# Another order for the pieces of a mixing block: equal turns and alternating quarters

## The chip, the cores and the metric

The kernel runs on one core of one Trainium2 chip. A core has a matrix engine (TensorE, "PE" in the profile; "PEld" is its weight load, which overlaps the matmuls), a vector engine (VectorE, "DVE"), an activation engine (ScalarE, "ACT"), a general engine (GpSimd, "POOL") and SyncE ("SP"), whose queue issues the DMA transfers here. The engines run side by side and wait for each other through semaphores. The metric is device microseconds of one execution, smaller is better.

## The reference, cut to what matters

A sequence of 512 tokens of width 1024 goes through two models' blocks. The first block has a mixing part and a mixture of experts; two attention layers with feed-forward parts follow. The edit concerns only the mixing part of the first block, which has two branches on the same normalised input `h`:

```python
a_x, a_gate, hy, gates = jnp.split(h @ w_in[l], [...], axis=-1)
xa = dwconv(a_x, conv_a_w[l], ...)
h_a = rg_lru(xa, ..., False) + rg_lru(xa, ..., True)
y_a = (h_a * gelu(a_gate)) @ w_a_out[l]
v, x1, x2 = jnp.split(dwconv(hy, conv_b_w[l], ...), 3, axis=-1)
filt = hyena_filters(S, ...)
z = v
for n, gate in enumerate((x1, x2)):
    z = gate * fftconv(z, bidir_kernel(filt[:, n, 0], filt[:, n, 1]), filt_bias[l, n])
y_b = z @ w_b_out[l]
g_a, g_b = jnp.split(sigmoid(gates), 2, axis=-1)
x = x + (g_a * y_a + g_b * y_b) @ w_o[l]
```

Branch A is a gated linear recurrence in both directions. Branch B multiplies spectra twice: a long convolution over the sequence with a filter, a gate, a second long convolution, a second gate. `g_a` and `g_b` are the sixteen output gates, 128 columns each.

## The kernel before, in words

Activations lie with channels on the partitions, 128 channels by 512 tokens a tile. A projection (`proj`, line 952) makes one such tile from `h`: eight blocks of 128 input channels, each with three matmuls of 128x512 (`mm3`, lines 163 to 165), since every f32 operand is split into a high and a low half (`hh`, `hl` of the input, `wh`, `wl` of the weight) and high x high, high x low and low x high are summed. `WStream.get` (line 217) loads the weight by DMA into one of three raw buffers (line 228), ScalarE copies the high half (line 152), DVE subtracts it to get the low half (line 155); there are two buffers of each half. Three PSUM banks take projections.

The code of the mixing part walks two lists of short words.

List A (line 845, loop at line 1166), for eight tiles of 128 channels, named by their number:

- `i`: projection of branch A's input, its short convolution on DVE (line 1126), high and low half of it.
- `r`: the recurrence. Twelve matmuls, tanh and exp on ScalarE, products and two scans on DVE (lines 1143 to 1162); it multiplies into `c.x`.
- `f`: one quarter of one filter: matmuls, then a product with the decay on DVE into `fs` (line 1260).
- `t`: transform of that filter: 24 short matmuls against a table `dft` (line 1197), sums and differences on DVE, and a store of the spectrum (line 1270).
- `G`: one output gate: projection, tanh (line 963), store (line 964). The digit is hexadecimal.

List B (line 846, loop at line 1413), for four quarters of 256 channels (first digit) and two steps (second digit):

- `c`: projection of one tile of `v`, `x1` or `x2` (second digit 0, 1, 2; third digit which of the two tiles), with its short convolution on DVE (line 1292).
- `u`: transposes on TensorE (line 1304) that bring `v` or `x1` into the order of time, copied by ScalarE.
- `L`: one long convolution: forward transform (line 1197), then some two dozen DVE instructions, among them the products with the filter's spectrum `K` (lines 1327 to 1353), which a DMA loads into one buffer (line 1391).
- `M`: inverse transform (line 1365). After step 0 DVE multiplies by the gate (line 1374); after step 1 the result is transposed back and gated (line 1387) into `c.x`.
- `y`: splits two of branch A's result tiles into halves (`yah`, `yal`); `A`: one tile of branch A's output projection, with its gate (line 1409), stored.

Behind list B branch B's result is split (`ybh`, `ybl`) and the output projections follow.

The lists aren't the order of instructions. A planner takes the program in the lists' order as priorities and gives each engine, by its own estimates of durations, the first instruction in that order that it holds ready and whose buffers are free; each engine then executes its instructions in the planned order and waits where one isn't ready. So a list sets which work has the right of way.

Of the kernel before, what the change touches and what calls it, by code (L numbers as in the profile page):

```python
# [841 lines left out]

STEPS_A = "i0 G8 i1 r0 f0 t0 i2 f2 r1 t2 f1 t1 i3 f3 r2 i4 G1 r3 i5 G0 r4 G2 i6 t3 r5 f4 t4 G4 f5 t5 f6 G7 i7 r6 t6 f7 G3 G5 r7 Gb t7 G6"
STEPS_B = "c000 c001 c020 c010 c120 c200 c011 u00 c100 c101 u01 L00 y0 c201 M00 c110 u10 u20 c220 L01 c111 u11 y1 L10 c021 c121 M01 M10 y2 L11 c300 M11 c301 c320 L20 y3 c210 c211 A0 c321 c310 u21 u30 A1 M20 c311 A2 L21 A3 L30 A4 Gf u31 c221 M21 A5 M30 Ga A6 L31 A7 M31 Ge Gc G9 Gd"
CFG1 = dict(acc=3, c=2, f=3, hA=0, lA=1, gh=0, gl=1, hB=0, lB=1, kh=0, kl=1, xh=0, xl=1, wl=1, rA=1, rX=1, bl=0, tA=5, tB=5, cv=8, U=4, u=2, th=5, fA='vvvv', fB='vvvv', gB='vvvv', hB2='vvvv', xg=1, K=1)
ACTDVE, POOLDVE = ("act", "dve"), ("pool", "dve")
MAGIC = 12582912.0
# [259 lines left out]
def recurrence(c, A, h, proj, lp, ps_c, ps_f, hb, sp, spd, quarter, dft, HS, HS0):  # L1109
# [55 lines left out]
    ins, fs = {}, {}  # L1165
    for s in STEPS_A.split():
        n = int(s[1], 16)
# [108 lines left out]
def branch_b(c, A, h, proj, ps_c, ps_f, bp, dft):  # L1276
# [135 lines left out]
    cv, us, ys = {}, {}, {}  # L1412
    for s in STEPS_B.split():
        if s[0] in "yA":
# [403 lines left out]
```

## Time and profile before

| | us |
|---|---|
| median of 3 runs | 2952.5 (2951.36 to 2955.3) |
| profiled execution | 2954.03 |
| its span, first to last instruction | 2952.2 |
| TensorE busy in the span | 2791.5 (95%) |
| VectorE busy | 1545.0 (52%) |
| ScalarE busy | 922.0 (31%) |
| mean granted TensorE clock | 0.984 |

The span has about three parts: the mixing part (list A from 60 us, list B from about 263 us to about 558 us, output projections behind), the experts, and the two attention layers. In the views that follow, a row of the view by stretches gives, for each engine, the busy time and the number of instructions, then the granted clock of TensorE as a mean over the stretch, the DMA engines' share and the rate. A row of the order of time gives start, duration, engine, line, operation, output and inputs, and in brackets how long the engine was idle before it and what ended that. A row of the waits gives total, count and longest. A row of groups gives busy time and the mean of one in ns.

### The profile page before, as it was taken

How to read it: one execution, taken by the hardware profiler on the slowest of the kernel's cores; microseconds unless marked ns; L12 is line 12 of the kernel's file. 1: busy time of each engine (PE TensorE's matmuls, PEld its weight loads, DVE VectorE, ACT ScalarE, POOL GpSimd, SP SyncE). 2: the span in 40 equal slices, each digit the busy share in tenths (PEclk: the TensorE clock that was granted, in tenths of full speed). 3: DMA queues.
4: the chain of work that ended last, by engine and by line, in shares of the span. 5: the costliest groups of instructions: out<-in, count | busy, mean ns of one | idle time of the engine just before them, and what ended most of it. 6: DMA issues, size and time to landing. Idle time of an engine off the chain costs nothing.

```text
span 2952.2 us, 35034 instructions
## 1 busy us (share of the span) xinstructions
PE 2791.5 (95%) x13300; PEld 1847.5 (63%) x13300; DVE 1545.0 (52%) x3121; ACT 922.0 (31%) x1553; POOL 177.6 (6%) x150
## 2 busy tenths in 40 slices
PE   8999989999999999998898899999999999999998
PEld 6778868773333333333334676688887776688887
DVE  7987798632222222222114789654435788654436
ACT  5565322321000000000002367443323377433324
POOL 0000000000000000000000233100000333000000
PEclk9999999999999999999999899999999999999999
DMA  4344224489999999999997223233223232223224
GB/s 167 130 139 152 93 89 151 157 290 394 421 420 420 421 420 421 420 421 420 421 420 307 80 77 85 75 101 100 93 94 120 92 83 76 85 93 100 93 94 135
DMA packets 136352, 617.89 MB, mean 209 GB/s; under 512 B 17423, under 2 KB 31575, under 8 KB 84600
## 3 DMA queue, kind: packets, MB, share of 16 engines
q1 hardware_dynamic: 136184, 615.65, 55.5%
q8 instruction: 105, 1.72, 0.2%
q14 instruction: 63, 0.52, 0.1%
HBM read 582.03 MB, written 16.78 MB: 203 GB/s over the span
## 4 chain that ended last, share of the span: by engine, by line
PE 76%; DVE 10%; DMA 7%; issue 4%; ACT 2%; POOL 1%; SPq 0%; DVEq 0%; ACTq 0%; POOLq 0%
PE gps L1665 11%; PE acc L165 10%; PE acc L164 10%; PE acc L163 10%; PE dps L1690 6%; DMA ew<-experts 5%; PE S L163 4%; PE S L164 4%; PE S L165 4%; PE o L615 2%; PE fps L1197 2%; PE acc L1618 2%; PE acc L1717 2%; PE S L549 2%; PE tp L598 1%
## 5 line engine op out<-in xcount | busy, mean ns | idle before, releaser
L152 ACT CAST wh<-wr 128x1024 fp32r<-128x1024 f32 (+3 forms) x294 | 291.6, 992 | 818.6 <-PE acc L164 520.3
L1665 PE MATMUL gps<-ew,xe 128*64 128x512 f32 x2048 | 488.8, 597 | 9.1 <-DMA ew<-experts 9.1
L155 DVE TENSOR_TENSOR wl<-wr,wh 128x1024 fp32r<-128x1024 f32 (+3 forms) x291 | 336.3, 1156 | 76.0 <-ACT wh L152 75.0
L1665 PEld LDWEIGHTS gps<-ew,xe 128*64 128x64 f32 x2048 | 151.1, 137 | 285.7 <-issue 254.6
L165 PE MATMUL acc<-hh,wl 128*128 128x512 f32 x768 | 308.9, 403 | 14.5 <-DVE wl L155 14.3
L163 PE MATMUL acc<-hh,wh 128*128 128x512 f32 x768 | 313.0, 408 | 2.2 <-DVE xa L1126 1.1
L164 PE MATMUL acc<-hl,wh 128*128 128x512 f32 x768 | 310.3, 404 | 0.0
L1690 PE MATMUL dps<-ew,hT 128*64 128x512 f32 x992 | 225.2, 600 | 15.2 <-DMA ew<-experts 8.7
L164 PE MATMUL acc<-fl,wh 128*128 128x512 f32 (+1 forms) x576 | 213.3, 370 | 0.0
L165 PE MATMUL acc<-fh,wl 128*128 128x512 f32 (+1 forms) x576 | 213.2, 370 | 0.0
L163 PE MATMUL acc<-fh,wh 128*128 128x512 f32 (+1 forms) x576 | 212.8, 370 | 0.0
L165 PE MATMUL S<-hh,wl 128*128 128x512 f32 x512 | 200.0, 391 | 0.0
L164 PE MATMUL S<-hl,wh 128*128 128x512 f32 x512 | 198.9, 389 | 0.0
L163 PE MATMUL S<-hh,wh 128*128 128x512 f32 x512 | 198.9, 389 | 0.0
L1673 DVE TENSOR_TENSOR g<-g,gps 128x512 f32<-128x512 f32 x32 | 21.9, 685 | 331.3 <-PE gps L1665 322.5
L165 PEld LDWEIGHTS acc<-hh,wl 128*128 128x128 f32 x768 | 147.4, 192 | 48.7 <-DVE wl L155 16.9
L163 PEld LDWEIGHTS acc<-hh,wh 128*128 128x128 f32 x768 | 148.0, 193 | 40.4 <-issue 7.9
L1690 PEld LDWEIGHTS dps<-ew,hT 128*64 128x64 f32 x992 | 74.9, 138 | 156.3 <-issue 128.1
L164 PEld LDWEIGHTS acc<-hl,wh 128*128 128x128 f32 x768 | 147.7, 192 | 32.4 <-issue 4.1
L395 DVE TENSOR_TENSOR x<-acc,x 128x512 f32<-128x512 f32 x56 | 38.7, 692 | 184.1 <-PE acc L165 184.1
L1672 ACT ACTIVATE g<-gps 128x512 f32<-128x512 f32 x32 | 19.2, 599 | 365.9 <-PE gps L1665 353.5
L379 DVE SCALAR_TENSOR_TENSOR r<-S,rsb 128x512 f32<-128x512 f32 x64 | 44.1, 692 | 162.2 <-PE S L165 158.5
(401 smaller groups left out, 4501.6 us busy)
## 6 DMA issues: line engine op xcount, KB each, us to landing
ew<-experts SPq DMA_DIRECT2D x384, 1024.0 KB, 19.8
wr<-w_down SPq DMA_DIRECT2D x72, 512.0 KB, 3.3
wr<-w_up SPq DMA_DIRECT2D x64, 512.0 KB, 3.3
wr<-w_in SPq DMA_DIRECT2D x56, 512.0 KB, 3.5
wr<-in_w SPq DMA_DIRECT2D x38, 512.0 KB, 3.4
R<-qkc SPq DMA_DIRECT2D x72, 128.0 KB, 2.3
filters_dram<-K SPq DMA_DIRECT2D x8, 1024.0 KB, 5.4
K<-filters_dram SPq DMA_DIRECT2D x8, 1024.0 KB
```

The lines of the kernel that those rows point to most:

```text
L152: nc.scalar.copy(hi, src)
L155: (nc.vector if lo_eng == "dve" else nc.gpsimd).tensor_tensor(lo, src, hi.bitcast(F32), op=OP.subtract)
L163: nc.tensor.matmul(ps, W[0], X[0], start=start, stop=False)
L164: nc.tensor.matmul(ps, W[0], X[1], start=False, stop=False)
L165: nc.tensor.matmul(ps, W[1], X[0], start=False, stop=stop)
L549: nc.tensor.matmul(ps, q[:, qs], k[:, ks], start=a == 0, stop=a == len(passes) - 1)
L615: nc.tensor.matmul(o[s * 64:(s + 1) * 64, q], v[:, j, vc[s]:vc[s] + 64], pts[s][:, a], start=a == 0, stop=a == len(js) - 1)
L1197: nc.tensor.matmul(ps[:, half * Q:(half + 1) * Q], dft[:, s], v[:, r], start=True, stop=True)
L1618: nc.tensor.matmul(ps[h * 64:(h + 1) * 64], sel[:, i], rows[i][h], start=i == 0, stop=i == 3)
L1665: nc.tensor.matmul(ps[h * 64:(h + 1) * 64], xes[e][:, kt], W[:, k, h * T:(h + 1) * T], start=kt == 0, stop=kt == 7)
L1690: nc.tensor.matmul(outs[e][col * 64:(col + 1) * 64], hT[:, j, p * 64:(p + 1) * 64], W[:, p, h * T:(h + 1) * T], start=cc == 0 and j == 0 a ...
L1717: nc.tensor.matmul(ps, Y[f // 4][j][:, (f % 4) * 128:(f % 4 + 1) * 128], st[f // 4], start=j == 0, stop=j == n - 1)
```

## The change

Only the two lists change. List A held ten of the sixteen gates and list B six; afterwards list A holds all sixteen. The new list A has eight turns, each of one input projection for the next turn, one filter, one recurrence, one transform and two gates (the last one differs at its ends). In the old one recurrences, filters and transforms come in uneven groups, and most gates stand in its second half. The new list B starts its first long convolution after four convolved tiles (before: nine) and takes the long convolutions in the order 00, 10, 01, 11, 20, 30, 21, 31, each pair of quarters alternating, with two convolved tiles and up to one output tile between most neighbours. The old one ends with four gates behind the last inverse transform, the new one with one output tile. No instruction is added or taken away, and no buffer count changes.

```diff
-STEPS_A = "i0 G8 i1 r0 f0 t0 i2 f2 r1 t2 f1 t1 i3 f3 r2 i4 G1 r3 i5 G0 r4 G2 i6 t3 r5 f4 t4 G4 f5 t5 f6 G7 i7 r6 t6 f7 G3 G5 r7 Gb t7 G6"
-STEPS_B = "c000 c001 c020 c010 c120 c200 c011 u00 c100 c101 u01 L00 y0 c201 M00 c110 u10 u20 c220 L01 c111 u11 y1 L10 c021 c121 M01 M10 y2 L11 c300 M11 c301 c320 L20 y3 c210 c211 A0 c321 c310 u21 u30 A1 M20 c311 A2 L21 A3 L30 A4 Gf u31 c221 M21 A5 M30 Ga A6 L31 A7 M31 Ge Gc G9 Gd"
+STEPS_A = "i0 G0 G1 i1 f0 r0 t0 G2 i2 f1 r1 t1 G3 G4 i3 f2 r2 t2 G5 G6 i4 f3 r3 t3 G7 G8 i5 f4 r4 t4 G9 Ga i6 f5 r5 t5 Gb Gc i7 f6 r6 t6 Gd Ge f7 r7 t7 Gf"
+STEPS_B = "c000 c001 u00 c010 c011 u01 y0 L00 c100 c101 u10 y1 M00 c020 c021 L10 y2 y3 c110 c111 u11 M10 c200 c201 L01 A0 c120 c121 u20 M01 L11 c210 c211 A1 M11 u21 c300 c301 L20 c220 c221 u30 A2 M20 L30 c310 c311 A3 u31 M30 L21 c320 c321 A4 M21 L31 A5 A6 M31 A7"
```

## The prediction

> **What bounds the kernel now.** I read the page's slices first, then busy time by stretches of the mixing block, then the waits and the order of work at the stretches where TensorE falls short.
>
> ```profile
> span 2952.2 us, 35034 instructions
> ...
> PE   8999989999999999998898899999999999999998
> ```
>
> The edit touches only the stretch from the first recurrence projection (60 us) to the first output product of branch B (559 us): slices 1 to 7, where TensorE's digit is 9 but for two.
>
> ```profile
> core 0: us, PE busy (x) PEld busy (x) DVE busy (x) ACT busy (x) POOL busy (x), PEclk, DMA share, GB/s
> 60.00:112.00 52.00, 52.00 (x235) 42.66 (x235) 47.83 (x82) 39.95 (x55) 0.00 (x0) 1.00 0.44 141
> 112.00:142.00 30.00, 23.17 (x94) 16.30 (x93) 28.44 (x46) 12.79 (x19) 0.00 (x0) 0.93 0.29 101
> 142.00:170.00 28.00, 27.84 (x109) 22.45 (x110) 18.47 (x29) 19.34 (x26) 0.00 (x0) 0.89 0.40 127
> 170.00:196.00 26.00, 22.99 (x99) 17.28 (x99) 23.93 (x40) 19.63 (x26) 0.00 (x0) 1.00 0.32 112
> 196.00:263.00 67.00, 66.16 (x302) 53.89 (x301) 58.17 (x92) 38.19 (x52) 0.00 (x0) 1.00 0.46 153
> ...
> 313.00:343.00 30.00, 29.54 (x137) 24.46 (x137) 28.15 (x38) 8.93 (x13) 0.00 (x0) 1.00 0.29 99
> 343.00:389.00 46.00, 39.02 (x170) 31.93 (x169) 41.10 (x56) 11.70 (x19) 0.00 (x0) 0.89 0.25 84
> 389.00:439.00 50.00, 45.87 (x207) 36.86 (x206) 46.67 (x64) 14.53 (x21) 0.00 (x0) 0.97 0.26 91
> ...
> 466.00:513.00 47.00, 47.00 (x218) 39.38 (x217) 45.44 (x61) 13.17 (x18) 0.00 (x0) 1.00 0.44 151
> 513.00:559.00 46.00, 43.59 (x195) 35.05 (x193) 32.74 (x45) 12.18 (x18) 0.26 (x2) 1.00 0.35 121
> 60.00:263.00 203.00, 192.16 (x835) 152.57 (x835) 176.84 (x285) 129.90 (x176) 0.00 (x0) 0.97 0.40 134
> 263.00:559.00 296.00, 282.02 (x1264) 231.81 (x1262) 238.87 (x318) 87.28 (x122) 0.26 (x2) 0.98 0.35 121
> ```
>
> The last two rows are stage A (list A) and stage B (list B). TensorE loses time in two ways: it is idle, or its clock is cut. Stage A: 203 - 192.2 = 10.8 idle, and 0.07 of 30 plus 0.11 of 28 = 5.2 of clock, so 16.0; its work needs 187.0. Stage B: 296 - 282.0 = 14.0, and 0.11 of 46 plus 0.03 of 50 = 6.6, so 20.6; need 275.4. The two losses, 36.6 us, are all that another order can win. They lie at 112 to 142, 170 to 196 and 343 to 439, where DVE is 89 to 95% busy. TensorE waits there for a low half of a weight:
>
> ```profile
> 369.56 1.05 ACT L152 CAST wh<-wr 128x1024 fp32r<-128x1024 f32 x1
> ...
> 379.82 1.21 DVE L155 TENSOR_TENSOR wl<-wr,wh 128x1024 fp32r<-128x1024 f32 x1
> ...
> 381.09 0.80 PE L165 MATMUL acc<-hh,wl 128*128 128x512 f32 x1 [6.96 <-DVE wl L155]
> ...
> PE acc L165 <- DVE wl L155: 13.2, 3, 7.0
> ...
> PE fps L1197 <- DVE fs L1260: 2.8, 4, 1.7
> ```
>
> ScalarE had the high half ready at 370.6; DVE came to the low half 9.2 us later, because work of two long convolutions stood before it.
>
> The Trainium skill ("TensorE: Matmul & The Clock Gate", What's actually happening) says the clock halves after at least one idle window of about 3.4 us. Here it is cut after less:
>
> ```profile
> 122.09 0.47 PE L163 MATMUL acc<-hh,wh 128*128 128x512 f32 x1 [1.14 <-DVE xa L1126]
> ...
> 124.00:128.00 4.00, 4.00 (x12) 2.97 (x12) 3.01 (x6) 1.41 (x2) 0.00 (x0) 0.57 0.23 69
> ```
>
> By the rule stage A's 5.2 us of clock would not follow from such short waits, the gain below would be 5.2 smaller and the time 2945.8; here no such result gets a chance, since the row shows the cut.
>
> **The change part by part.** Nothing is added or removed; 56 projections, 8 recurrences, filters, transforms, 8 long convolutions stay. Six gates (9, a, c, d, e, f) move from stage B to stage A. One projection's price:
>
> ```profile
> 285.31 1.23 DVE L155 TENSOR_TENSOR wl<-wr,wh 128x1024 fp32r<-128x1024 f32 x1 [2.77 <-ACT wh L152]
> ...
> 290.75 1.23 DVE L155 TENSOR_TENSOR wl<-wr,wh 128x1024 fp32r<-128x1024 f32 x1 [2.77 <-ACT wh L152]
> ```
>
> TensorE was full there, so 24 matmuls take 290.75 - 285.31 = 5.44 us. The rest by kinds:
>
> ```profile
> L155 DVE TENSOR_TENSOR wl<-wr,wh 128x1024 fp32r<-128x1024 f32 x39 | 47.5, 1219 | 35.7 <-ACT wh L152 35.5
> ...
> L1292 DVE SCALAR_TENSOR_TENSOR x<-acc,p,x 128x511 f32<-128x511 f32 x32 | 23.7, 743 | 0.2
> ...
> L1409 DVE SCALAR_TENSOR_TENSOR ga<-ga,acc 128x512 f32<-128x512 f32 x8 | 5.5, 683 | 5.9 <-PE acc L165 4.0 <-DMA wr<-w_in 1.9
> ...
> L963 ACT ACTIVATE gate<-acc 128x512 f32<-128x512 f32 x7 | 4.1, 591 | 3.7 <-issue 3.7
> L152 ACT CAST wh<-wr 128x1024 fp32r<-128x1024 f32 x39 | 41.0, 1052 | 164.1 <-PE acc L164 139.6 <-issue 24.4
> ```
>
> A gate costs DVE 1.22, ScalarE 1.05 + 0.59, a convolved tile 1.22 + 2 x 0.74 = 2.7 of DVE, an output tile 1.22 + 0.68 = 1.9. Six gates carry 32.6 us of TensorE, 7.3 of DVE and 9.8 of ScalarE to stage A. ScalarE goes from 130 of 203 to 140 of 220 and is no bound: it ran at 40 of 52 (first row) with TensorE full. New needs: stage A 219.6 with DVE 184.2, 84%; stage B 242.8 with DVE 231.6, 95%.
>
> Stage A, equal turns. The nearest row is 196 to 263, where most old gates stand: DVE 87% busy, TensorE idle 0.84 of 67, or 1.3%; of 219.6 that is 2.8. New is that transform follows filter within each turn, with only a recurrence between. The wait for the filter (L1260) cost 2.8 in four cases, 0.7 each; eight are 5.6. Bounds of the loss: 0, and 2.8 + 8 x 1.7 (the longest) = 16.4. I take 5.6, the middle of 2.8 and 8.4. Gain 16.0 - 5.6 = 10.4, from -0.4 to 16.
>
> Stage B, fewer projections around the same DVE work. The first long convolution now stands behind four convolved tiles, not nine.
>
> ```profile
> L1197 PE MATMUL fps<-u,dft 128*128 128x256 f32 x128 | 30.4, 383 | 0.0
> L1365 PE MATMUL cps<-U,dft 128*128 128x256 f32 x128 | 29.3, 382 | 0.0
> ...
> L1304 PE MATMUL cps<-ident,v 128*128 128x128 f32 x32 | 4.9, 287 | 0.2 <-ACT xg L1318 0.2
> ```
>
> Its spectrum is done after 4 x 5.44, two sets of transposes (4.9/4 each, 2.5) and 30.4/8 = 3.8: 28.1 us. DVE has in that time four tiles (10.8) and the eight splits of the recurrence's result (2.48 for four, 5.0), which run early now although three quarters of them are listed later:
>
> ```profile
> 272.09 2.48 DVE L155 TENSOR_TENSOR yal<-x,yah 128x512 fp32r<-128x512 f32 x4
> ...
> 557.35 4.25 ACT L152 CAST ybh<-x 128x512 fp32r<-128x512 f32 x8
> ...
> 558.01 0.50 PE L163 MATMUL acc<-ybh,wh 128*128 128x512 f32 x1 [1.91 <-ACT ybh L152]
> ```
>
> So 231.6 - 15.8 = 215.8 of DVE remain. In the stretches with convolutions (313 to 439, 466 to 513) it was busy 161.4 of 173, 93.3%: 231.3 us. The seam to the next stage waited for the split of branch B's result (1.91 in the last row, some 2.5 with what follows); today four gates run after the last convolution, now one output tile (5.44) lies beside its inverse (29.3/8 = 3.7), which hides it; uncovered it would add those 3.7. The stage takes 28.1 + 231.3 + 2.5 = 261.9, against 296 - 32.6 = 263.4 for the same work in the old order: gain 1.5. The best stretch (45.44 of 47, 96.7%) gives 253.8, gain 9.6; the worst (41.10 of 46, 89.3%) 272.3, a loss of 8.9. I take the mean, since the new list has both kinds of neighbourhood.
>
> **DMA queues.** All loads and stores issue on SP in the planned order. Each moved gate takes its weight load and its store along, past the filters' decay loads; late ones would lengthen the filter wait, whose longest is in the lower bound. Stage B has one buffer for a filter spectrum:
>
> ```profile
> SPq L1391 <- DVE U L1328: 30.0, 7, 6.8
> ```
>
> While that load waits for the previous product, weight loads stand behind it. Three raw buffers covered this (no TensorE wait named a load above), so I cost it at nothing; without cover it is up to 6.8 per convolution.
>
> **The sum.** Span 2952.2; the profiled execution took 2954.0. 2954.0 - 10.4 - 1.5 = 2942.1 for such an execution. The median of the runs is 2952.5, 1.5 below it: 2940.6.
>
> **Rivals.** *Starved weights, slower.* One convolution on DVE:
>
> ```profile
> 522.96 0.69 DVE L1206 TENSOR_TENSOR sa<-fps,so 128x512 f32<-128x512 f32 x1 [0.28 <-ACT so L1203]
> ...
> 543.15 0.68 DVE L1353 TENSOR_TENSOR U<-U 128x512 f32<-128x512 f32 x1
> ```
>
> These are the first and last of 24; less two low halves and one output product between them, 543.83 - 522.96 - 3.1 = 17.8. In the new list most convolutions stand two convolved tiles and one output tile apart: DVE needs 17.8 + 5.4 + 1.9 = 25.1, TensorE 3 x 5.44 + 1.2 + 3.8 + 3.7 = 25.0. No margin: a second chain starts while the first runs, and low halves wait behind both, as at 379.8. The place is L01/L11 and L20 through L31. The price of one is 6.98 idle and 5.1 of clock (343 to 389), 12.1. Three make 36.3, with the seam 38.8 in place of 20.6: 18.2 lost, less 10.4 won in stage A, +7.8: 2960.3. It decides from the third stall; two leave the forecast. For it: stage B has DVE at 95% of the need, where 343 to 439 fell short. Against: 466 to 513 ran at 97% without idling.
>
> The Trainium skill ("TensorE: Matmul & The Clock Gate", Architectural detail) says VectorE takes its instructions strictly in order; the 9.2 us of the low half agree.
>
> *One stage pays the other.* Stage B at its worst, -8.9, eats the 10.4: 2951.0. The list also only ranks work: the eight early splits show that the planner moves it far, so the issued order could change less than the text does, and the time stays too.
>
> *Both stages fill.* Stage A loses only 2.8 (gain 13.2), B runs at 96.7% (9.6): 2929.7.
>
> **How the numbers follow.** Forecast 0.42 (its own range 2932 to 2946), both fill 0.16, one pays the other 0.17, starved 0.25. What a measurement can tell from no change is 0.2%, 5.9 us. Faster 0.42 + 0.16 = 0.58, same 0.17, slower 0.25. Bounds of the costs: 2952.5 - 16 - 9.6 = 2926.9 and 2952.5 + 0.4 + 8.9 = 2961.8. The range takes these in, with a little below for a seam without wait: 2924 to 2962; left out are perhaps 0.03 below and 0.12 above (four starved stalls).
>
> **What would show it.** Stage A: the gap at 112 to 142 gone, clock 1.00 throughout, waits of L1197 for L1260 about 5 us, length near 225. Stage B: DVE busy above 90% from the first spectrum to the last, length near 262. Wrong would be: low-half waits over 4 us, with the clock cut behind them, at neighbouring convolutions, DVE in stage A still near 95% in a stretch, or a TensorE wait that names a load.

## The result and the profile after

| | before | after |
|---|---|---|
| median | 2953.35 us (4 runs, 2951.36 to 2955.3) | 2930.08 us (4 runs, 2928.11 to 2932.4) |
| ratio to before | | 0.9926, interval 0.9914 to 0.9939 |
| span of the profiled execution | 2952.2 | 2926.6 |
| from the first projection of list A to the first output product of branch B | 498.2 | 470.2 |

The kernel became faster: the medians differ by 23.3 us, about twice the forecast of 12, and the ratio is clear of 1. First the page's slices, then busy time by stretches of the changed kernel; the last two rows are its stage A and stage B.

```profile
span 2926.6 us, 35016 instructions
...
PE   8999999999999999998898899999999999999998
```

```profile
60.00:112.00 52.00, 51.92 (x231) 41.63 (x230) 42.31 (x70) 33.89 (x47) 0.00 (x0) 1.00 0.47 156
112.00:142.00 30.00, 29.99 (x135) 24.08 (x134) 25.01 (x40) 19.87 (x28) 0.00 (x0) 1.00 0.48 164
142.00:196.00 54.00, 53.02 (x239) 43.04 (x238) 42.82 (x69) 32.25 (x44) 0.00 (x0) 1.00 0.43 149
196.00:281.00 85.00, 84.43 (x381) 68.62 (x381) 71.19 (x112) 53.74 (x72) 0.00 (x0) 1.00 0.37 130
...
304.00:331.00 27.00, 27.00 (x127) 22.44 (x126) 26.20 (x36) 9.25 (x14) 0.00 (x0) 1.00 0.29 98
331.00:406.00 75.00, 74.64 (x342) 61.96 (x341) 68.89 (x94) 21.18 (x29) 0.00 (x0) 1.00 0.29 99
406.00:504.00 98.00, 97.73 (x448) 81.23 (x447) 93.30 (x128) 29.23 (x39) 0.26 (x2) 1.00 0.39 134
504.00:531.00 27.00, 23.46 (x101) 17.86 (x99) 24.12 (x35) 5.65 (x9) 0.00 (x0) 0.94 0.30 105
531.00:560.00 29.00, 27.14 (x111) 21.63 (x110) 18.98 (x27) 10.14 (x15) 0.00 (x0) 0.94 0.54 178
60.00:281.00 221.00, 219.35 (x981) 177.38 (x980) 181.33 (x288) 139.75 (x188) 0.00 (x0) 1.00 0.42 146
281.00:531.00 250.00, 245.83 (x1120) 202.72 (x1118) 229.29 (x313) 78.95 (x109) 0.26 (x2) 0.99 0.36 124
```

The holes at 112 to 142, 170 to 196 and 343 to 439 have gone: up to 504 us TensorE is idle 2.3 us in all, at full clock. What is left is the end of list B, 504 to 531, where a weight's low half comes 2.2 us late between the last convolution's VectorE instructions and TensorE then waits 0.6 us for the convolution itself, and the seam behind it. The largest waits of TensorE from 60 to 560 us (total, count, longest) say the same:

```profile
PE acc L165 <- DVE wl L155: 4.1, 5, 2.2
PE acc L164 <- DVE ybl L155: 1.9, 1, 1.9
PE cps L1365 <- DVE U L1349: 0.6, 1, 0.6
PE acc L163 <- ACT wh L152: 0.5, 1, 0.5
```

The low halves of weights, 13.2 us before with a longest of 7.0, cost 4.1; the filter products (L1260) no longer appear.

To compare stages, I put the border where the first convolved tile's projection starts: its copy by ScalarE comes at 268.9 before and at 286.8 after. I took 5.9 and 5.4 us in front of it for the projection, so 263.0 and 281.4; by the order of the matmuls in the traces this is good to about 0.3 us.

```profile
286.83 0.78 ACT L1289 ACTIVATE v<-acc,p 128x512 f32<-128x512 f32 x1
```

Stage A went from 203.2 to 220.7 us with 32.6 us of gates more: 15.1 us won. Stage B went from 295.0 to 249.5 with 32.6 less: 12.9 won. Together that is 28.0 us. Outside the two stages 2.4 us were given back: list A starts 0.9 us later (60.7 for 59.8), and the part behind the first output product takes 2395.7 us for 2394.2, which leaves the 25.6 us between the two spans. That part is 4.5 us longer up to the experts' first matmul (120.4 for 115.9), where the seam's low half comes later, and 3.0 us of it come back from there on. Rows from about 1 us behind the first output product to the end, before and after:

```profile
559.00:2952.00 2393.00, 2266.37 (x10997) 1424.40 (x10997) 1084.00 (x2416) 669.69 (x1209) 176.88 (x143) 0.99 0.60 228
```

```profile
532.00:2926.00 2394.00, 2266.70 (x10996) 1425.12 (x10996) 1085.06 (x2418) 670.02 (x1209) 176.82 (x143) 0.98 0.59 227
```

### The profile page after: what moved, and what is told of

Same layout as the page of the kernel before. It is cut to its first block, busy times and chain, and to the rows that moved or that the text cites. A ratio compares the mean times of both kernels' runs of the same rounds, so it can differ in the third digit from the quotient of the medians.

```text
span 2926.6 us, 35016 instructions
## 1 busy us (share of the span) xinstructions
PE 2782.9 (95%) x13300; PEld 1844.3 (63%) x13300; DVE 1541.2 (53%) x3121; ACT 923.7 (32%) x1553; POOL 177.5 (6%) x150
## 4 chain that ended last, share of the span: by engine, by line
PE 78%; DMA 8%; DVE 8%; issue 3%; ACT 1%; POOL 1%; SPq 0%; DVEq 0%; ACTq 0%; POOLq 0%
PE acc L165 11%; PE acc L164 11%; PE acc L163 11%; PE gps L1665 11%; DMA ew<-experts 8%; PE dps L1690 5%; PE S L163 4%; PE S L164 4%; PE S L165 4%; PE fps L1197 2%; PE o L615 2%; PE acc L1717 2%; PE acc L1618 2%; PE S L549 2%; PE tp L598 1%
```

## The experiments

All change only the two lists. "Both stages" is the time from the first projection of list A to the first output product of branch B in the profiled execution; it holds the same work in every run. Each ratio is to runs of the kernel before that were taken with that experiment (their medians lie between 2951.9 and 2955.4).

| run | median us | ratio to before, interval | both stages | A / B |
|---|---|---|---|---|
| before | 2953.35 | | 498.2 | 203.2 / 295.0 |
| after | 2930.08 | 0.9926, 0.9914 to 0.9939 | 470.2 | 220.7 / 249.5 |
| e1_newA_oldB | 2961.37 | 1.0026, 1.0017 to 1.0036 | 504.4 | 221.0 / 283.4 |
| e2_oldA_newB | 2937.74 | 0.9950, 0.9936 to 0.9965 | 480.0 | 201.4 / 278.6 |
| e3_gates_last | 2950.84 | 0.9996, 0.9986 to 1.0005 | 492.9 | 244.4 / 248.4 |
| e4_in_turn | 2942.86 | 0.9964, 0.9953 to 0.9976 | 484.6 | 221.4 / 263.1 |
| e5_late_first | 2951.00 | 0.9995, 0.9985 to 1.0004 | 493.0 | 221.3 / 271.6 |
| e6_paired | 2959.63 | 1.0026, 1.0016 to 1.0036 | 501.8 | 221.6 / 280.2 |
| e7_oldA_even | 2922.02 | 0.9893, 0.9879 to 0.9908 | 466.1 | |
| e8_two_behind | 2928.66 | 0.9919, 0.9904 to 0.9934 | 472.2 | |
| e9_turns_ten | 2924.81 | 0.9901, 0.9881 to 0.9920 | 467.7 | 189.1 / 278.6 |

Before, e2, e7 and e9 hold six gates (32.6 us) in B, e8 two, the others none. In e7 and e8 the first convolved tiles' projections run among the last turn's matmuls, and their copies come late (in e7 the first projection starts at about 241.8 us, its copy at 258.2), so no border can be drawn there.

**One list at a time.** e1 is the new list A with the old list B, its gates left out:

```diff
-c000 c001 u00 c010 c011 u01 y0 L00 c100 ... A6 M31 A7
+c000 c001 c020 c010 c120 c200 c011 u00 c100 c101 u01 L00 ... u31 c221 M21 A5 M30 A6 L31 A7 M31
```

> List A as changed (all sixteen gates, equal turns), list B in the old order without its six gates. Theory 1 (two separate gains: stage A about 14 us from gates spread evenly, stage B about 13 us from the new order): stage A 221 us as in the changed kernel, stage B 263 us or more, since the old order keeps its late first convolution and its paired convolutions and has lost six gates of cover; about 2940 us. Theory 2 (all of the gain comes from where the gates stand, the order of branch B gives nothing): about 2930 us.

Both theories missed the time: the kernel became slower than before. Stage A is 221.0, as expected, but stage B, for which theory 1 had said 263 or more, is 283.4, where the old order with its gates took 295.0 - 32.6 = 262.4. The gates had covered 21 us of that order's waits. TensorE's waits in its stage B, and the stretch behind the first spectrum:

```profile
PE cps L1365 <- DVE U L1349: 15.5, 1, 15.5
PE acc L165 <- DVE wl L155: 10.5, 2, 6.9
```

```profile
331.80:565.00 233.20, 203.29 (x888) 165.48 (x887) 201.81 (x273) 56.06 (x79) 0.26 (x2) 0.93 0.30 108
```

The last inverse waits 15.5 us for VectorE with no projection left to run, and the two old starved weights are still there, with the clock at 0.93. So moving the gates without the new order of branch B costs more than stage A wins.

e2 is the old list A with the new list B, the six gates put back at their old places:

```diff
-STEPS_A = "i0 G0 G1 i1 f0 r0 t0 G2 ... t7 Gf"
+STEPS_A = "i0 G8 i1 r0 f0 t0 i2 f2 ... t7 G6"
-... c320 c321 A4 M21 L31 A5 A6 M31 A7
+... c320 c321 A4 Gf M21 L31 A5 Ga A6 M31 A7 Ge Gc G9 Gd
```

> List A as before (ten gates), list B in the new order, with the six gates at the places that they have in the old list B (behind A4, behind A5, four at the end). Theory 1: stage A keeps its 203 us with the gap at 112 to 142; stage B, 32.6 us longer by the gates, is 13 us or more below the 296 of before; about 2939 us. Theory 2: no gain in stage B, about 2953 us.

Theory 1 holds: 2937.7. Stage A keeps most of its loss (201.4 for 203.2); stage B, 278.6 - 32.6 = 246.0 net, is 16.4 us below the old order. Rows of its stage A and B:

```profile
60.00:262.60 202.60, 191.40 (x840) 151.52 (x840) 178.21 (x286) 131.61 (x178) 0.00 (x0) 0.99 0.40 136
262.60:541.00 278.40, 276.06 (x1261) 228.34 (x1259) 235.16 (x314) 85.96 (x119) 0.26 (x2) 1.00 0.36 127
```

**Stage A: what about the gates.** e3 puts all gates behind the turns.

```diff
-i0 G0 G1 i1 f0 r0 t0 G2 i2 ... t7 Gf
+i0 i1 f0 r0 t0 i2 f1 r1 t1 i3 ... f7 r7 t7 G0 G1 G2 G3 G4 G5 G6 G7 G8 G9 Ga Gb Gc Gd Ge Gf
```

> As the changed kernel, but list A's sixteen gates all stand behind its eight turns. Theory 1 (the place of the gates in the list is the place where they run): turns without a gate are bound by VectorE, some 162 us of work at 95%, then 87 us of gates on TensorE alone: stage A some 255 us, about 2963 us. Rival (the list only ranks; the planner pulls gates that are ready forward into TensorE's gaps): within 5 us of the changed kernel, 2930 to 2935 us.

Measured between the two: stage A 244.4, 23.7 longer than with even gates.

```profile
60.00:245.00 185.00, 164.54 (x718) 130.63 (x718) 170.88 (x281) 124.55 (x168) 0.00 (x0) 0.95 0.37 131
245.00:305.00 60.00, 60.00 (x266) 49.70 (x265) 13.54 (x12) 17.16 (x24) 0.00 (x0) 1.00 0.41 146
```

While the turns run, VectorE is 92% busy and TensorE idles 20.5 us; then TensorE is full and VectorE has little to do (13.5 of 60). The first gate's tanh runs at 202.5 us, 37 us before the gates run one behind the other (from 239.5): the planner pulled three gates forward, but not enough to undo the list.

e7 keeps the old order of inputs, recurrences, filters and transforms and its ten gates, and only spreads these evenly; list B is that of e2.

```diff
-i0 G8 i1 r0 f0 t0 i2 f2 r1 t2 f1 t1 i3 f3 r2 i4 G1 r3 ... Gb t7 G6
+i0 G8 i1 r0 f0 t0 G1 i2 f2 r1 t2 G0 f1 t1 G2 i3 f3 r2 G4 i4 r3 i5 G7 r4 i6 t3 r5 G3 f4 t4 f5 t5 G5 f6 i7 r6 t6 Gb f7 r7 t7 G6
```

> List A with its old order of inputs, recurrences, filters and transforms, but its ten gates spread evenly; list B as in the run with old A and new B (2937.7 us). Theory G (stage A lost its time in turns without gates): the 16 us of loss fall to 6 or less, 2926 to 2931 us. Rival (the uneven groups of filters and transforms cost it, or ten gates are too few whatever their place): 2935 to 2940 us.

Theory G holds, and goes further than it said: 2922.0 lies below its 2926 to 2931, and the run is the fastest of all, ratio 0.9893. Against e2 only the gates' places differ, and the gain is 15.7 us between the medians (13.9 in both stages of the profiled executions), about what stage A won in the change. TensorE is idle 5.1 us in all, for 13.5 in e2:

```profile
60.00:253.00 193.00, 190.47 (x862) 155.70 (x861) 177.37 (x285) 131.97 (x178) 0.00 (x0) 1.00 0.41 143
253.00:526.00 273.00, 270.41 (x1237) 223.93 (x1235) 235.38 (x317) 84.68 (x117) 0.26 (x2) 1.00 0.36 128
```

e9 gives the equal turns of the change one gate each, with the same list B.

```diff
-i0 G0 G1 i1 f0 r0 t0 G2 i2 f1 r1 t1 G3 G4 ... t7 Gf
+i0 G0 i1 f0 r0 t0 G1 i2 f1 r1 t1 G2 i3 f2 r2 t2 G3 ... f7 r7 t7 G8 Gb
```

> The equal turns of the changed kernel with one gate each (ten in list A, the last two behind the eighth turn), list B as in the run with old A and new B (six gates). Theory G (in stage A only the even place of the gates counts, the order within the turn does not): as the run with the old order and its ten gates spread evenly, 2920 to 2925 us. Rival (equal turns add a gain of their own, or with one gate a turn VectorE binds): below 2918 us, or 2928 us and more.

2924.8, its interval overlapping that of e7: the equal turns add nothing to the even gates that these runs could show. Here the border is clean: stage B takes 278.6 us as in e2, and stage A is 12.3 us shorter than there, which is the whole gain in the two stages (480.0 to 467.7).

**Stage B: start, pairs, alternation.** Each of the next three was meant to change one property of the new list B, under the new list A. e5 starts the first convolution behind nine tiles.

```diff
-c000 c001 u00 c010 c011 u01 y0 L00 c100 c101 u10 y1 M00 c020 c021 L10 y2 y3 c110 c111 u11 M10 ...
+c000 c001 c010 c011 c100 c101 c020 c021 c110 u00 u01 y0 L00 u10 y1 M00 L10 y2 y3 c111 u11 M10 ...
```

> As the changed kernel, but nine convolved tiles stand before the first long convolution, as in the old list B; alternation and spacing behind it stay. Theory S (start: VectorE has little to do until the first spectrum, and what it misses there is missing at the end, where TensorE has run out of projections): five tiles more give 5 x (5.44 - 2.7) = 13.7 us of idle VectorE, the wait before the last inverse grows by about that, 2938 to 2946 us. Rival P (pairs of adjacent convolutions were what cost stage B): 2928 to 2934 us.

Stage B is 22.1 us longer, more than theory S said (2951.0 us, behind its 2938 to 2946), and not in the place it named. TensorE's largest waits in its stage B, and the stretch behind the first spectrum:

```profile
PE acc L165 <- DVE wl L155: 11.2, 5, 5.0
PE cps L1365 <- DVE U L1349: 4.1, 1, 4.1
```

```profile
333.90:554.00 220.10, 201.33 (x883) 163.71 (x881) 196.96 (x271) 55.44 (x77) 0.26 (x2) 0.95 0.31 109
```

The wait before the last inverse grew by 3.5 us, from 0.6 to 4.1. In all TensorE is idle 18.8 us, for 4.2 in the change; the largest part of that is starved low halves (11.2): with the same VectorE work packed into fewer projections, the halves stood behind it. The rest of the 22.1 is clock: the same matmuls keep TensorE busy 252.8 us in the stage, for 245.4 in the change. The edit also leaves fewer tiles between L00, L10 and L01, so it mixes a late start with tighter spacing, and doesn't tell these two apart.

e6 starts as early as the change, but puts six convolutions in three adjacent pairs.

```diff
-... M00 c020 c021 L10 y2 y3 c110 c111 u11 M10 c200 c201 L01 A0 ...
+... M00 L10 L01 c020 c021 y2 y3 c110 c111 u11 M10 c200 c201 A0 M01 u20 L11 L20 ... u30 L30 L21 ...
```

> As the changed kernel, with the first long convolution as early, but the middle six in three adjacent pairs (10 01, 11 20, 30 21), the convolved tiles gathered behind each pair. Theory P (a pair starves the weights' low halves): three stalls of 7 us with some 5 us of clock, 2950 to 2966 us. Theory S (the early start is what counts, the planner spreads the rest): 2930 to 2936 us.

Theory P holds: stage B is 280.2, 30.7 us longer.

```profile
PE acc L165 <- DVE wl L155: 12.6, 3, 8.4
PE cps L1304 <- DVE x L1292: 7.9, 1, 7.9
PE cps L1365 <- DVE U L1349: 3.7, 1, 3.7
```

There is one stall at each pair: 7.9 us for the short convolution of a tile (at 362 us), 4.0 and 8.4 us for a low half (at 425 and 488), all queued on VectorE behind the pair.

e4 takes both convolutions of a quarter one after the other, with the same spacing.

```diff
-... L00 ... L10 ... L01 ... L11 ... L20 ... L30 ... L21 ... L31
+... L00 ... L01 ... L10 ... L11 ... L20 ... L21 ... L30 ... L31
```

> As the changed kernel, but list B takes the long convolutions of each quarter one after the other (00, 01, 10, 11, 20, 21, 30, 31) with the same two convolved tiles and output tile between them. Theory 1 with alternation as its cause: after each first convolution VectorE has no spectrum to work on until the inverse and the next forward transform are done, some 8 us in each of four quarters, of which convolved tiles fill a part; 15 to 25 us longer, 2945 to 2955 us. Rival (spacing and the early start are enough, alternation does nothing): 2928 to 2934 us.

Stage B is 13.6 us longer, a little under the expectation (2942.9 for 2945 to 2955). Its two largest waits:

```profile
PE cps L1365 <- DVE U L1349: 5.9, 1, 5.9
PE acc L165 <- DVE wl L155: 5.0, 6, 1.4
```

The first is the wait for the last convolution, the second low halves in six small waits. Alternation counts, but less than keeping the convolutions apart (e6).

**The rest of the end.** e8 takes two gates from list A to the last convolution.

```diff
-... i7 f6 r6 t6 Gd Ge f7 r7 t7 Gf
+... i7 f6 r6 t6 Gd f7 r7 t7
-... L31 A5 A6 M31 A7
+... L31 A5 Ge A6 Gf M31 A7
```

> As the changed kernel, but the last two gates leave list A and stand between the output tiles beside the last long convolution (L31 A5 Ge A6 Gf M31 A7). Theory S: TensorE has run out of projections there (some 7 us lost from 504 to 531 us, and the clock cut behind it), two gates fill that and stage A gets 10.9 us shorter: 2923 to 2927 us. Rival (VectorE sets the end, two more low halves only lengthen it): 2930 us or more.

2928.7 lies between the two, and its interval overlaps that of the change. The hole was filled, but the waits came back elsewhere:

```profile
504.00:531.00 27.00, 26.25 (x118) 21.31 (x118) 20.28 (x29) 7.59 (x10) 0.26 (x2) 1.00 0.44 159
270.00:532.00 262.00, 256.34 (x1167) 210.53 (x1165) 238.18 (x327) 82.25 (x113) 0.26 (x2) 1.00 0.34 121
```

TensorE idles 0.75 from 504 to 531, yet 5.7 from 270 to 532. Why e2's six gates leave only 2.3 there and two don't help was not settled.

## Why the prediction was right or wrong

**What bounds the kernel.** The two losses, 36.6 us, were named as the most that another order could win; the change won 28.0 of them in the two stages, and the best run 32.1. Their places were the right ones, but two readings of them were not. In stage A the low half of a projection's weight is only 2.6 of the 13.2 us of such waits; the rest of its idle time is nearly all waits for other results of VectorE, the filter (2.8) first among them. And 2.2 us of stage B are counted twice, as idle time and as clock: around the wait of 6.96 us at 381.1 the granted clock was 0.61 from 376 to 379 and 0.50 from 379 to 381, while TensorE stood idle, and 0.50 to 0.52 from 381 to 387. Only the last part slowed matmuls; it cost 2.9 us, not 5.1. So a starved weight of that size costs about 9.9 us in place of 12.1, and about 34 us were there to be won.

**Stage A: the general loss about right, the filter waits mis-sized.** The gain was 15.1, forecast 10.4, within its bounds of -0.4 and 16. The general loss is a little below what the row of 196 to 263 gave: TensorE idle 1.65 us, where 2.8 was taken. Eight waits on the filter (L1260) were priced at 5.6 us, and half of that, 2.8, went into the sum; none occurred: the list of waits has none. I took the list's order for TensorE's order; in the trace a projection's matmuls run between a filter's and its transform's (at 108 to 115 us, for instance). e7 and e2 show the cause: with nothing but the places of the gates changed, 15.7 us. The equal turns themselves are no part of it (e9).

**Stage B: the step that failed.** I took 93.3%, the mean busy share of VectorE in stretches with convolutions, as the rate at which the rest of its work would be done. The stage took 12.4 us less than the 261.9. Rows of the changed kernel, up to the first spectrum and from there:

```profile
281.40:307.30 25.90, 25.90 (x122) 21.67 (x121) 19.32 (x27) 15.27 (x23) 0.00 (x0) 1.00 0.56 197
307.30:531.00 223.70, 219.53 (x998) 180.74 (x996) 209.58 (x286) 63.28 (x86) 0.26 (x2) 0.99 0.34 116
```

The spectrum came after 25.9, not 28.1 (2.2 us). VectorE had done 19.3 by then, not 15.8 (2.4 of the 19.3 are the end of the last filter's transform, which fell behind the border), and did 228.9 in the stage, not 231.6, so 209.6 were left for 215.8 (6.2 at 0.933: 6.6 us). The share was 93.7% (1.0 us), and the seam's 2.5 us fell behind the first output product, which started before the split was done. These four make 12.3. By this sum the terms that were mis-sized are the work left to VectorE and the seam. But that the share came out right doesn't make it a rate: in the runs above, the same work behind the first spectrum ran at 201.81 of 233.20 (87%, e1), and in e2 at 235.16 of 278.40 over the stage with TensorE full. The share is a result of the order. In the old kernel two of the four stretches it was averaged from had TensorE full (29.54 of 30, 47.00 of 47); there VectorE was busy 73.6 of 77 us (96%) and idled because TensorE set the pace, and I counted this as a loss of VectorE. In the other two, where TensorE starved, it was busy 87.8 of 96 (91%). The mean mixes two limits and is the rate of neither. What sets the changed stage B is TensorE's own need: 242.8 by the forecast's count, 245 with the clock counted once, 249.5 measured; the row of 250 us shows TensorE busy for 245.8.

**DMA queues.** No wait of TensorE names a load, as costed.

**The rivals.** "Both stages fill" (2929.7) described the result best; both of its gains, 13.2 and 9.6, were passed, by 5.2 us together. That its time fits the 2930.1 to 0.4 us is in part luck: 2.4 us were given back outside the stages, and the rest of the 5.2 lies in the spread between single runs and medians. "Starved weights" named a real mechanism, and e6 is nearly that case: 2959.6, where the rival said 2960.3. The sum fits better than its parts: the rival had three stalls of 12.1 and the seam, e6 has five waits of over 1 us (8.4, 7.9, 4.0, 3.7 and 1.3). It doesn't happen in the changed list because the convolutions aren't adjacent: 25.1 us of VectorE against 25.0 of TensorE between two starts is no margin, but also no deficit. That a list only ranks is half true: in e3 the planner ran the first gate 37 us ahead of the row of gates, and the run still lost 21 us against the change. "One stage pays the other" didn't occur in the change; the run that shows something like it is e1, where the old list B lost 21 us once its gates were gone.

**What would show it.** The gap at 112 to 142 closed and the clock was 1.00 in stage A, as said; its length was 220.7, not 225. VectorE stayed above 90% in nearly all of stage B; its length was 249.5, not 262.

## What to carry to other kernels

Where two engines are both near full, read which of them is idle in each stretch before taking a busy share as a rate: a share that was averaged over stretches in which the other engine was full says nothing of how fast the first can go. Matmuls that depend on nothing nearby are cover: spread them evenly over the stretches in which VectorE has the most work per projection, and don't take them from a stage whose own order still needs them (e1). Keep long VectorE chains a few projections apart, since a weight's low half that queues behind two of them stops TensorE.

## What the runs showed of the hardware

The clock is cut after short waits, and not after each. In the changed kernel the waits of 0.50 and 2.15 us at 510 to 513 are followed by slower matmuls (0.59 and 0.63 in place of 0.39), 1 us after work had resumed; the granted clock is 0.72 from 514 to 520:

```profile
510.51 0.50 PE L163 MATMUL acc<-yah,wh 128*128 128x512 f32 x1 [0.50 <-ACT wh L152]
510.85 0.40 PE L164 MATMUL acc<-yal,wh 128*128 128x512 f32 x1
513.40 0.50 PE L165 MATMUL acc<-yah,wl 128*128 128x512 f32 x1 [2.15 <-DVE wl L155]
...
514.43 0.59 PE L163 MATMUL acc<-yah,wh 128*128 128x512 f32 x1
514.82 0.63 PE L164 MATMUL acc<-yal,wh 128*128 128x512 f32 x1
```

The seam behind list B has the same two waits, 1.9 and 0.6 us, in the kernel before and in e7 (here e7's):

```profile
PE acc L163 <- ACT ybh L152: 1.9, 1, 1.9
...
PE acc L164 <- DVE ybl L155: 0.6, 1, 0.6
```

The granted clock is 1.00 in the first (555 to 580) and 0.94 in the second (520 to 550, with 0.50 from 528 to 530):

```profile
555.00:580.00 25.00, 22.52 (x96) 17.78 (x95) 15.59 (x22) 10.75 (x16) 0.00 (x0) 1.00 0.65 203
```

```profile
520.00:550.00 30.00, 27.52 (x112) 21.82 (x111) 16.52 (x26) 10.74 (x16) 0.00 (x0) 0.94 0.60 196
```

So the price of a wait of about 2 us here is the wait, and in some places up to 0.06 of 30, 1.8 us, of clock more. What decides between the two was not found. A low clock costs time only while TensorE works: of the 5.1 us that 0.11 of 46 make at 343 to 389 in the kernel before, 2.2 fell into the wait itself.
